# A hybrid decoder layer on one core: a first stage in program order with the statistics behind further products, and the attention heads' norm placed into the last retention projection

## The chip, the cores and the metric

The kernel runs on one core of a Trainium2 chip. The metric is the device time of one execution in microseconds (us), of which the median of several runs counts; less is better. TensorE (PE) multiplies matrices, VectorE (DVE), ScalarE (ACT) and GpSimd (POOL) work on rows of 128 partitions, and SyncE (SP) issues most of the transfers (DMA).

## The reference

All is float32: 1024 rows of 1024 columns, 16 meta rows ahead of them. Of the layer this matters here:

```python
u = rmsnorm(h, norm1_w[l])                  # over the 1024 columns
proj = u_pad @ w_in[l]                      # 1024 x 11264
rq, rk, rv, rg, dq, dk, dv, gates = jnp.split(proj, SPLIT_IDX, axis=-1)
rq = rope(rq, ...); rk = rope(rk, ...)      # 4 retention heads
ro = retention(rq, rk, rv)                  # chunks of 128, a state per head
ro = (silu(rg) * normed(ro)) @ w_ret_o[l]
dq = rope(rmsnorm(dq, q_norm_w[l]), ...)    # 8 attention heads, two halves of 64
dk = rope(rmsnorm(dk, k_norm_w[l]), ...)
do = diff_attention(dq, dk, dv, lam)
do = rmsnorm(do, diff_subln_w[l]) * (1.0 - lam_init)
do = do @ w_diff_o[l]
mix = (sigmoid(g_ret) * ro + sigmoid(g_diff) * do) @ w_out[l]
h = h + mix                                 # then a gated MLP with a convolution
```

## The kernel before, in words

Everything lies transposed, channels on the 128 partitions and up to 1040 positions along them, in groups of 346 to 348 columns (`KG`, three for 1040) or 342 (`QG`, three for 1026). Each float32 operand is split into a high and a low part of a shorter type; a product is three matmuls (high by high, high by low, low by high). A **unit** is half of a group of a projection: 12 matmuls. Weight tiles of 128 output channels come in two halves of 128x512 through a ring of three raw buffers (`raw_half`, tag `wr`); ScalarE makes the high part and GpSimd the low one (`split_half`).

*The start.* `norm_in` (L382) loads the eight input tiles `xT[k]`, multiplies each with its column of the norm's weight and splits it (`uh`, `ul`, both on VectorE), squares it on ScalarE and adds the squares up on VectorE and GpSimd. `kouter` (L198) multiplies the first two weight tiles, the keys and queries (`dk`, `dq`) of attention head 0, with input tile after input tile as they come: 8 x 18 = 144 matmuls into six accumulators. The root mean square itself is put in later: `stats` sums over partitions with TensorE, `rms` spreads the result (`rb`) and multiplies it into the rotation tables `cosr` and `sinr`, on GpSimd; the values' evacuation multiplies with `rb`. `evacuate` squares keys and queries and rotates them group by group; their own statistics go to DRAM and come back spread over the partitions. `defer(n, f)` calls `f` after n ticks, a tick being a unit or a group of `kouter`. `lam` makes a scalar from four small loads.

*The middle.* `phase1` writes the heads' steps between units of the projections (`blend`): 60 units go to each of the eight attention heads, and what is left over fills the first retention head. Head 0 begins with `prepare`, which splits keys and queries and moves halves between partitions by nine transfers that GpSimd issues. The tiles that fill are `rk`, `rq`, `rv`, `rg` and the gates, in the order of the list `fill`. `phase2` runs four retention heads, each with the output projection (`ret_out`) of the head before among its steps.

*The end of it.* The last head's `ret_out` (24 groups of 12 matmuls) runs after 2 groups and `ret_tail` (the last chunk's gate, transposes and splits). Its groups use two accumulators (`acc`), which VectorE frees by an addition (L961). `phase3` (L979) loads what the eight attention heads left in DRAM (`do`) and a row of statistics spread over the partitions, multiplies them (L990) and splits the product (ScalarE L242 and L247, the low part of odd heads on GpSimd).

The order on the engines is set by a scheduler, which takes instructions by their dependences and may move them ahead of others, except within `manual_schedule`, where they stay as written; the kernel before has no such part here.

## Time and profile before

| what | us |
|---|---|
| median of 3 runs (2581.33 to 2583.19) | 2583.08 |
| the profiled execution | 2585.65 |
| its span | 2583.9 |
| TensorE busy in the span | 2515.7 |
| VectorE, ScalarE, GpSimd busy | 1576.3, 900.5, 856.9 |
| mean granted clock of TensorE | 0.991 of full speed |

The profile follows one execution. A row of a timeline gives the start, the duration, the engine, the line of the kernel, the operation with what it writes and reads, and in brackets how long the engine had been idle and what released it. Rows of the stretches give each engine's busy time with its instructions in brackets (PE, then PEld, the loading of weights, DVE, ACT, POOL), then the mean granted clock while TensorE worked.

### The profile page before, as it was taken

The numbers are of one execution on the slowest core, as the hardware profiler recorded it, in microseconds if no ns is written. First come the engines' busy times: TensorE is split into PE (matmuls) and PEld (weight loads), VectorE is DVE, ScalarE is ACT, GpSimd is POOL, SyncE is SP. The second block draws the span as 40 slices with busy tenths as digits, with TensorE's granted clock in tenths as the row PEclk, the third lists the DMA queues.
The fourth block names the chain that finished last, engine by engine and source line by source line (L and its number), as shares of the span: only waits on it lengthen the run. The fifth ranks groups of instructions, "written<-read, shape, count | busy, mean of one in ns | idle before, by whom it ended". The sixth has DMA issues, their size and how long they took to land.

```text
span 2583.9 us, 40473 instructions
## 1 busy us (share of the span) xinstructions
PE 2515.7 (97%) x15444; PEld 2415.7 (93%) x15444; DVE 1576.3 (61%) x3239; ACT 900.5 (35%) x1881; POOL 856.9 (33%) x668
## 2 busy tenths in 40 slices
PE   7999999999999999999999998999999999999999
PEld 6888998999999999999999998999999999999998
DVE  8576766556474746453787888352466555555555
ACT  4244434354343434342556553232311111111111
POOL 4433343323232222212333432444333333332332
PEclk8999999999999999999999998999999999999999
DMA  4423141424233241424443443523111111111112
GB/s 176 104 74 98 55 130 62 127 83 115 84 89 98 68 116 55 129 78 114 116 106 89 108 104 115 175 87 115 41 50 49 42 49 50 50 41 50 50 50 86
DMA packets 171538, 224.55 MB, mean 87 GB/s; under 512 B 26712, under 2 KB 109264, under 8 KB 171344
## 3 DMA queue, kind: packets, MB, share of 16 engines
q1 hardware_dynamic: 165440, 202.70, 25.9%
q0 software_dynamic: 5760, 19.17, 3.7%
q8 instruction: 121, 1.98, 0.3%
q14 instruction: 73, 0.60, 0.1%
q10 hardware_dynamic: 144, 0.10, 0.0%
HBM read 160.20 MB, written 42.35 MB: 78 GB/s over the span
## 4 chain that ended last, share of the span: by engine, by line
PE 80%; DVE 10%; issue 4%; ACT 3%; DMA 2%; POOL 2%; SPq 0%; DVEq 0%; POOLq 0%; ACTq 0%
PE acc L175 46%; PE sc L175 26%; PE ot L175 3%; PE st L175 2%; DVE b L499 1%; PE sc L640 1%; DVE b L501 1%; ACT b L624 1%; DMA b<-d 1%; DVE b L617 1%; DVE sh L498 1%; POOL wl L230 1%; DVE b L253 1%; DVE sql L247 1%; DVE b L247 1%
## 5 line engine op out<-in xcount | busy, mean ns | idle before, releaser
L175 PE MATMUL acc<-b,wh 128*128 128x342 f32 (+3 forms) x6076 | 1481.3, 326 | 27.2 <-DVE b L961 6.8
L175 PEld LDWEIGHTS acc<-b,wh 128*128 128x128 f32 x6076 | 1055.2, 190 | 42.6 <-DVE b L961 7.4
L175 PE MATMUL acc<-b,wl 128*128 128x342 f32 (+3 forms) x3038 | 986.5, 325 | 0.3 <-POOL wl L230 0.3
L230 POOL TENSOR_TENSOR wl<-wr,wh 128x512 fp32r<-128x512 f32 x370 | 520.4, 1425 | 1044.5 <-ACT wh L227 1031.5
L175 PE MATMUL sc<-b,wh 128*128 128x342 f32 (+2 forms) x2452 | 616.7, 334 | 0.0
L175 PEld LDWEIGHTS acc<-b,wl 128*128 128x128 f32 x3038 | 576.0, 190 | 5.9 <-POOL wl L230 0.6
L175 PEld LDWEIGHTS sc<-b,wh 128*128 128x128 f32 x2452 | 433.3, 189 | 20.6 <-ACT wh L227 0.4
L227 ACT CAST wh<-wr 128x512 fp32r<-128x512 f32 x370 | 215.0, 618 | 571.9 <-issue 286.5
L175 PE MATMUL sc<-b,wl 128*128 128x342 f32 (+2 forms) x1226 | 410.3, 335 | 0.8 <-POOL wl L230 0.7
L247 POOL TENSOR_TENSOR b<-b,b 128x512 fp32r<-128x512 f32 (+2 forms) x90 | 147.5, 1639 | 320.1 <-ACT b L242 289.7
L175 PEld LDWEIGHTS sc<-b,wl 128*128 128x128 f32 x1226 | 232.1, 189 | 11.9 <-POOL wl L230 1.7
L242 ACT CAST b<-b 128x512 fp32r<-128x512 f32 (+2 forms) x135 | 100.1, 745 | 241.7 <-DVE b L1144 146.5
L534 DVE TENSOR_TENSOR ev<-acc,b 128x342 f32<-128x342 f32 (+1 forms) x144 | 74.1, 515 | 145.5 <-PE acc L175 124.9
L624 ACT ACTIVATE b<-b,sm 128x272 f32<-128x272 f32 (+7 forms) x128 | 100.9, 788 | 175.9 <-DVE sm L623 153.7
L1107 DVE SCALAR_TENSOR_TENSOR b<-b,cols,b 128x1024 f32<-128x1024 f32 x88 | 149.6, 1700 | 2.3
L617 DVE CUSTOM_DVE_ANT_0 b<-sc,consts 128x144 f32<-128x144 f32 (+6 forms) x224 | 106.6, 503 | 55.1 <-PE sc L175 54.9
L1098 DVE TENSOR_TENSOR b<-sc,b 128x342 f32<-128x342 f32 x84 | 42.5, 511 | 136.8 <-PE sc L175 136.8
L1122 DVE TENSOR_TENSOR b<-b,sc 128x512 f32<-128x512 f32 x117 | 78.6, 682 | 48.2 <-PE sc L175 48.2
L242 ACT CAST ah<-sc 128x512 fp32r<-128x512 f32 (+2 forms) x144 | 67.3, 468 | 105.2 <-PE sc L640 68.5
L247 DVE TENSOR_TENSOR al<-sc,ah 128x512 fp32r<-128x512 f32 (+2 forms) x144 | 77.3, 538 | 42.9 <-ACT ah L242 41.5
L500 POOL TENSOR_TENSOR sh<-sh,b 128x346 f32<-128x346 f32 (+1 forms) x48 | 49.9, 1040 | 152.4 <-DVE sh L498 146.2
L175 PE MATMUL sc<-b,b 128*128 128x264 f32 (+9 forms) x480 | 95.5, 317 | 4.8 <-DVE sm L617 4.7
(233 smaller groups left out, 2738.2 us busy)
## 6 DMA issues: line engine op xcount, KB each, us to landing
wr<-w_in SPq DMA_DIRECT2D x176, 256.0 KB
wr<-w_up SPq DMA_DIRECT2D x88, 256.0 KB
d<-ev SPq DMA_DIRECT2D x120, 171.0 KB
b<-b POOLq DMA_DIRECT2D x72, 260.0 KB, 4.3
b<-d SPq DMA_DIRECT2D x256, 64.0 KB
b<-d SPq DMA_DIRECT2D x24, 513.0 KB
wr<-w_down SPq DMA_DIRECT2D x44, 256.0 KB
b<-d SPq DMA_DIRECT2D x32, 260.0 KB
```

Source lines behind the costliest of these rows:

```text
L175: self.E.matmul(out, lhsT=l, rhs=r, start=start, stop=stop)
L227: self.A.copy(h, raw)
L230: self.G.tensor_sub(l, raw, h.bitcast(F32))
L242: self.A.copy(dh, src)
L247: (self.V if el == "V" else self.G).tensor_sub(dl, src, dh.bitcast(F32))
L500: G.tensor_mul(sh[:, :n], sh[:, :n], self.Sn[:, cs])
L534: V.tensor_mul(o[:, :n], ps[:, :n], self.rb[:, cs])
L617: V.tensor_tensor_reduce(out=sc_[:m, a0:a0 + sz], in0=ps[:m, :sz], in1=mk, scale=1.0, scalar=3e38, op0=ALU.add, op1=ALU.min, accum_out=sm[ ...
L624: A.activation(sc_[:m, :n], sc_[:m, :n], AF.Exp, bias=mx, scale=-1.0, accum_out=sm[:m, 10 + c:11 + c])
L1098: self.V.tensor_mul(up[:, t0:t0 + n], ps[:, :n], self.rb2[:, t0:t0 + n])
L1107: V.scalar_tensor_tensor(out=o[:, q], in0=up[:, NMETA - 2 + i:T - 2 + i], scalar=self.cw(i, fi), in1=o[:, q], op0=ALU.mult, op1=ALU.add)
L1122: self.V.tensor_add(h, h, ps)
```

## The change

`norm_in` and the first 15 units are written in the order in which they shall run. The raw weights of the first three tiles have buffers of their own; ScalarE makes the high part of seven of the inputs, VectorE the low parts of inputs and of these weights and all sums, and GpSimd has nothing to do there. `kouter` takes the first input tile's products kind by kind over its six accumulators. Keys and queries of head 0 are copied and squared on ScalarE out of the accumulators and then treated in whole rows of 1040; all statistics, rotations and `lam` are deferred behind units of the next tiles. The tiles `rv0` to `rv3` come first in the list. `prepare(0)` runs between units ahead of head 0, 5 units more follow, and a head has 58 units. The last `ret_out` has six accumulators, another order of its first six groups and `ret_tail` after four; the loads and the norm of the attention heads are written into it, and all low parts are VectorE's; `phase3` does without its loop over the heads.

```diff
+            three = lambda w: ((w[0], xh, k == 0, False), (w[0], xl, False, False), (w[1], xh, False, k == 7))
+            if k == 0:
+                order = [(three(w)[i], p, g) for i in range(3) for w, pg in zip(ws, ps) for p, g in zip(pg, groups)]
+            else:
+                order = [(t, p, g) for w, pg in zip(ws, ps) for p, g in zip(pg, groups) for t in three(w)]
+            for (w, x, b, e), p, (t0, n) in order:
+                self.mm(p[:, :n], w[:, k, :], x(k)[:, t0:t0 + n], b, e)
                 self.tick()
...
+        (self.G if el == "G" else self.V).tensor_sub(l, raw, h.bitcast(F32))
...
+        weights(0, 0, 1)
+        load(1, 2)
+        weights(4, 0, 1)
+        load(3, 4, 5, 6)
+        weights(0, 2)
+        load(7)
+        weights(4, 2)
+        self.const_loads()
+        self.C, self.Sn, self.cosr, self.sinr = (self.big() for _ in range(4))
+        for i, t in ((2, self.C), (3, self.Sn), (0, self.cosr), (1, self.sinr)):
+            S.dma_start(out=t, in_=self.a["trig"][i])
+        half = lambda b, i: self.split_half(ws[b], raws[b][:, i:i + 4, :], i, "V")
...
+        def low(k):
+            V.scalar_tensor_tensor(out=self.ul[k], in0=xs[k], scalar=self.n1[k], in1=self.uh[k].bitcast(F32),
+                                   op0=ALU.mult, op1=ALU.subtract)
+        sums = {2: [(0, 1)], 4: [(2, 3)], 5: [(0, 2)], 6: [(4, 5)], 7: [(0, 4), (0, 6)]}
...
-            self.split(uh, ul, x, eh="V", el="V", scale=self.n1[k])
...
-            A.activation(x, x, AF.Square)
-            if k == 1:
-                for w, r in zip(ws, raws[2:]):
-                    self.split_half(w, r, 4)
-            for e, i, j in {1: [(G, 0, 1)], 3: [(G, 2, 3), (G, 0, 2)], 5: [(V, 4, 5)], 6: [(V, 4, 6)],
-                            7: [(V, 4, 7), (V, 0, 4)]}.get(k, []):
-                e.tensor_add(xs[i], xs[i], xs[j])
-        self.loaded.append(self.load_w(self.stream.pop(0), [self.big(F32R)[:, :D].rearrange("p (a b) -> p a b", a=8) for _ in range(2)]))
-        self.constants()
+            if k == 0:
+                V.tensor_scalar(out=uh, in0=x, scalar1=self.n1[k], scalar2=None, op0=ALU.mult)
+                low(k)
+                half(0, 0)
+                half(1, 0)
+            else:
+                A.activation(uh, x, AF.Copy, scale=self.n1[k])
+                low(k)
+                A.activation(xs[k - 1], xs[k - 1], AF.Square)
+            if k == 2:
+                half(0, 4)
+                half(1, 4)
+            elif k == 6:
+                half(2, 0)
+            for i, j in sums.get(k, []):
+                V.tensor_add(xs[i], xs[i], xs[j])
+        A.activation(xs[7], xs[7], AF.Square)
+        half(2, 4)
+        self.const_cast()
+        V.tensor_add(xs[0], xs[0], xs[7])
...
-            x, *r = self.rstat(st, 348, 1.0 / 8, tag="x1")
+            x, *r = self.rstat(st, 348, 1.0 / 8, tag="x1", eh="V")
...
-        self.lam()
         ps = self.kouter(ws, lambda k: self.uh[k], lambda k: self.ul[k], KG)
-        self.defer(1, stats)
...
+        def trig():
             G.tensor_mul(self.cosr, self.cosr, self.rb)
             G.tensor_mul(self.sinr, self.sinr, self.rb)
...
-        self.defer(6, rms)
-        for kind, pg in zip(("dk", "dq"), ps):
-            for g in range(3):
-                self.evacuate(kind, 0, g, pg[g], KG, 4 + g//2 + 2 * (kind == "dq"))
+        kinds = ("dk", "dq")
+        raw = [self.big() for _ in kinds]
+        sq = [self.big() for _ in kinds]
+        for w, g in ((0, 0), (1, 2), (0, 1), (0, 2), (1, 0), (1, 1)):
+            t0, n = KG[g]
+            A.activation(raw[w][:, t0:t0 + n], ps[w][g][:, :n], AF.Copy, scale=self.qw if w else self.kw)
+            A.activation(sq[w][:, t0:t0 + n], ps[w][g][:, :n], AF.Square)
+        parts = [(self.big(F32R), self.big(F32R)) for _ in kinds]
+        def squares():
+            for w in range(2):
+                self.split(*parts[w], sq[w])
+        def rotate(*ws):
+            for w in ws:
+                sh = sq[w]
+                V.stream_shuffle(out=sh, in_=raw[w], mask=[(j + 8) % 16 if j < 16 else j for j in range(32)])
+                V.tensor_mul(raw[w], raw[w], self.C)
+                V.tensor_mul(sh, sh, self.Sn)
+                V.tensor_add(raw[w], raw[w], sh)
+        def stat():
+            st = self.st()
+            for w in range(2):
+                for g, (t0, n) in enumerate(KG):
+                    self.stat(st[:, :n], self.S6[2 * g + w], [t[:, t0:t0 + n] for t in parts[w]], w == 0 and g == 0, w == 1 and g == 2)
+            y = self.rstat(st, 348, eps=self.eps)
+            d = self.dram([4, T])
+            for j, (b0, m) in enumerate(KG):
+                S.dma_start(out=d[:, b0:b0 + m], in_=y[40 * j:40 * j + 40:10, :m])
+            self.ys[0] = d
+        def spread():
+            for w in range(2):
+                for r in (0, 64):
+                    S.dma_start(out=sq[w][r:r + 64, :], in_=self.ys[0][2 * w + r // 64:2 * w + r // 64 + 1, :].to_broadcast([64, T]))
+        def norm():
+            for w, kind in enumerate(kinds):
+                V.tensor_mul(raw[w], raw[w], sq[w])
+                self.raw[kind, 0] = raw[w]
+            self.normed.add(0)
+        for n, f in ((1, stats), (2, squares), (5, rms), (6, stat), (8, lambda: rotate(0)), (10, lambda: rotate(1)),
+                     (12, spread), (15, self.lam), (16, norm), (28, trig)):
+            self.defer(n, f)
...
+        fill = fill[16:20] + fill[:16] + fill[20:]
...
-        self.norm_in()
-        gen = self.projections(seq[2:])
-        units = 6 * (len(seq) - 2)
-        for _ in range(6):
+        with self.tc.manual_schedule():
+            self.norm_in()
+            gen = self.projections(seq[2:])
+            units = 6 * (len(seq) - 2)
+            for _ in range(15):
+                next(gen)
+                units -= 1
+        for _ in self.prepare(0):
             next(gen)
-        units -= 6
+            units -= 1
+        for _ in range(5):
+            next(gen)
+            units -= 1
         for h in range(DH):
-            n = 60
+            n = 58
             self.blend(self.attention(h), self.ATT_WEIGHT, gen, n)
             units -= n
...
+        last = h == RH - 1
+        order = [(m, g) for m in range(8) for g in range(3)]
+        if last:
+            order[:6] = [(0, 0), (0, 1), (1, 0), (1, 1), (0, 2), (1, 2)]
+        for m, g in order:
+            t0, n = QG[g]
+            if m % 2 == 0 and g == 0:
...
+            ps = self.acc6() if last else self.acc()
...
+        self.heads = []
+        for _ in range(4):
             next(prev)
         self.ret_tail()
-        for _ in prev:
-            pass
+        with self.tc.manual_schedule():
+            coming = [self.load_head(0)]
+            for i, _ in enumerate(prev):
+                if i % 3 == 0 and i < 20:
+                    coming.append(self.load_head(i // 3 + 1))
+                elif i % 3 == 2:
+                    self.norm_head(i // 3, *coming.pop(0))
+            while coming:
+                self.norm_head(len(self.heads), *coming.pop(0))
+    def load_head(self, h):
+        S = self.S
+        q = slice(HALO, T)
+        sp, sy = self.spill["do", h]
+        d, y = self.big(), self.big()
+        S.dma_start(out=d[:, q], in_=sp[:, q])
+        for p, n in enumerate((258, 256, 256, 256)):
+            t0 = HALO if p == 0 else NMETA + 256 * p
+            S.dma_start(out=y[:, t0:t0 + n], in_=sy[p:p + 1, :n].to_broadcast([P, n]))
+        return d, y
...
+    def norm_head(self, h, d, y):
+        q = slice(HALO, T)
+        self.V.scalar_tensor_tensor(out=d[:, q], in0=d[:, q], scalar=self.sw, in1=y[:, q], op0=ALU.mult, op1=ALU.mult)
+        a, b = self.big(F32R), self.big(F32R)
+        self.split(a[:, q], b[:, q], d[:, q])
+        self.heads.append((a, b))
...
+        dh, dl = ([t[i] for t in self.heads] for i in range(2))
+        self.heads = None
```

What stands in a row at the start of ScalarE's program, before and then after (`wh` are high parts of weights, L409 squares of inputs; in the second, L434 makes high parts of inputs, L436 squares, and `cols` are the weights of the norm):

```order
L322 DMA cols<-cols 128x195
L320 ACT_TABLE_LOAD
L320 ACTIVATE eps<-eps 128x1
L227 CAST wh_72<-wr_95 128x512
L227 CAST wh_74<-wr_97 128x512
L227 CAST wh_72<-wr_100 128x512
L227 CAST wh_74<-wr_108 128x512
L409 ACTIVATE b_76<-b_76 128x1040
```

```order
L319 ACT_TABLE_LOAD
L319 ACTIVATE eps<-eps 128x1
L321 DMA cols<-cols 128x195
L228 CAST wh_74<-b_88 128x512
L228 CAST wh_76<-b_89 128x512
L434 ACTIVATE b_141<-b_81,cols 128x1040
L436 ACTIVATE b_80<-b_80 128x1040
L434 ACTIVATE b_146<-b_82,cols 128x1040
```

The transfer of `cols` now stands behind the table load and the first activation, and high parts of inputs stand between the squares.

SyncE's transfers behind the first statistics, before and then after (`wr` are raw weights, L512 and L506 the stores of head 0's statistics, L518 and after it L512 their way back, L607 a store of the values):

```order
L430 DMA eps<-x_472 8x348
L221 DMA wr_592<-w_in 128x512
L221 DMA wr_704<-w_in 128x512
L221 DMA wr_708<-w_in 128x512
L221 DMA wr_833<-w_in 128x512
L512 DMA d_623<-ry_612 4x348
L512 DMA d_623<-ry_612 4x346 x2
L518 DMA b_654<-d_623 64x1040 x2
L518 DMA b_699<-d_623 64x1040 x2
```

```order
L462 DMA eps<-x_402 8x348
L506 DMA d_532<-ry_521 4x348
L506 DMA d_532<-ry_521 4x346 x2
L223 DMA wr_538<-w_in 128x512
L223 DMA wr_542<-w_in 128x512
L607 DMA d_571<-ev_572 128x348
L607 DMA d_571<-ev_604 128x346
L607 DMA d_571<-ev_636 128x346
L512 DMA b_354<-d_532 64x1040 x2
L512 DMA b_355<-d_532 64x1040 x2
```

The loads of raw weights stood ahead of the stores of the statistics; two of them now stand behind these stores.

VectorE's program in the last `ret_out`, before and then after (`acc` and `sc` are accumulators; L961 and after it L1043 are the additions, L913 and L990 the gate, L247 and L246 low parts, L990 and after it L1082 the product of an attention head):

```order
L961 TENSOR_TENSOR b_14508<-b_14508,acc_18118 128x342
L990 SCALAR_TENSOR_TENSOR b_18534<-b_18534,qkw,b_18535 128x1026
L961 TENSOR_TENSOR b_14508<-b_14508,acc_18132 128x342
L913 TENSOR_TENSOR vl_17882<-sc_18146,vl_17882 128x512
L247 TENSOR_TENSOR b_16868<-vl_17882,b_16864 128x128
L247 TENSOR_TENSOR b_16869<-vl_17882,b_16865 128x128
L247 TENSOR_TENSOR b_16870<-vl_17882,b_16866 128x128
L247 TENSOR_TENSOR b_16871<-vl_17882,b_16867 128x128
L961 TENSOR_TENSOR b_14508<-b_14508,acc_18160 128x342
L961 TENSOR_TENSOR b_14624<-b_14624,acc_18174 128x342
L990 SCALAR_TENSOR_TENSOR b_18546<-b_18546,qkw,b_18547 128x1026
L961 TENSOR_TENSOR b_14624<-b_14624,acc_18188 128x342
```

```order
L1043 TENSOR_TENSOR b_14580<-b_14580,sc_18116 128x342
L990 TENSOR_TENSOR vl_17838<-sc_18130,vl_17838 128x512
L246 TENSOR_TENSOR b_16824<-vl_17838,b_16820 128x128
L246 TENSOR_TENSOR b_16825<-vl_17838,b_16821 128x128
L246 TENSOR_TENSOR b_16826<-vl_17838,b_16822 128x128
L246 TENSOR_TENSOR b_16827<-vl_17838,b_16823 128x128
L1043 TENSOR_TENSOR b_14464<-b_14464,sc_18153 128x342
L1043 TENSOR_TENSOR b_14580<-b_14580,acc_18174 128x342
L1043 TENSOR_TENSOR b_14802<-b_14802,acc_18198 128x342
L1082 SCALAR_TENSOR_TENSOR b_18146<-b_18146,qkw,b_18147 128x1026
L246 TENSOR_TENSOR b_18214<-b_18146,b_18213 128x1026
L1043 TENSOR_TENSOR b_14802<-b_14802,sc_18217 128x342
```

The product of a head stood between two additions ahead of the last chunk's gate; now the gate and its four low parts come first, then three additions, then the first head's product.

## Rows read from the trace of the kernel before

**Rows 1.** The page's busy times: engine, us, share of the span, instructions.

```profile
PE 2515.7 (97%) x15444; PEld 2415.7 (93%) x15444; DVE 1576.3 (61%) x3239; ACT 900.5 (35%) x1881; POOL 856.9 (33%) x668
```

**Rows 2.** Stretches of the span: a:b, length, busy per engine, clock, DMA share, GB/s.

```profile
0.00:39.20 39.20, 29.21 (x144) 27.50 (x144) 33.56 (x27) 15.08 (x20) 19.11 (x13) 0.96 0.60 215
0.00:122.80 122.80, 100.53 (x545) 95.00 (x546) 89.31 (x116) 40.42 (x77) 59.34 (x49) 0.93 0.47 143
122.80:250.00 127.20, 117.59 (x745) 113.34 (x744) 92.48 (x233) 58.26 (x142) 47.57 (x47) 0.96 0.33 90
1572.00:1582.00 10.00, 7.21 (x24) 6.24 (x23) 7.85 (x23) 2.13 (x3) 3.70 (x3) 0.66 0.19 53
1600.00:1610.00 10.00, 7.72 (x31) 7.45 (x32) 4.30 (x8) 1.08 (x5) 2.36 (x1) 0.66 0.51 166
1602.80:1608.40 5.60, 5.55 (x19) 5.55 (x20) 1.11 (x4) 0.00 (x0) 0.00 (x0) 0.50 0.47 168
1610.00:1620.00 10.00, 10.00 (x65) 10.00 (x65) 4.65 (x7) 2.20 (x3) 2.55 (x2) 1.00 0.27 78
1620.00:1630.00 10.00, 5.98 (x28) 5.71 (x27) 2.13 (x3) 1.05 (x1) 2.38 (x1) 0.79 0.39 134
```

**Rows 3.** TensorE's waits, 0 to 123 us: waited for, total us, times, longest.

```profile
PE acc L175 <- DVE b L252: 6.4, 1, 6.4
...
PE acc L175 <- ACT x L471: 4.4, 1, 4.4
...
PE ot L175 <- DVE ryl L253: 1.4, 1, 1.4
```

**Rows 4.** The same view of 123 to 250 us.

```profile
PE sc L640 <- DVE b L631: 4.4, 2, 3.8
PE sc L676 <- DVE sm L617: 2.8, 1, 2.8
```

**Rows 5.** VectorE's timeline, 1565 to 1645: start, us, instruction, idle before it.

```profile
1569.97 4.17 DVE L247 TENSOR_TENSOR b<-x,b 128x128 fp32r<-128x128 f32 x4
...
1600.51 2.88 DVE L247 TENSOR_TENSOR b<-vl,b 128x128 fp32r<-128x128 f32 x4 [0.36 <-ACT b L242]
...
1624.67 1.29 DVE L990 SCALAR_TENSOR_TENSOR b<-b,qkw,b 128x1026 f32<-128x1026 f32 x1 [5.48 <-DMA b<-d]
```

**Rows 6.** SyncE's own timeline, 1570 to 1665.

```profile
1619.83 3.42 SPq L989 DMA_DIRECT2D b<-d  x4
```

**Rows 7.** ScalarE's timeline, 0 to 9 us (ACTq: a transfer that it issues).

```profile
0.74 0.41 ACTq L322 DMA_DIRECT2D cols<-cols  x1
1.18 1.28 ACT L320 ACT_TABLE_LOAD   x1 [1.18 <-PEq L1201]
```

**Rows 8.** VectorE's timeline, 0 to 104 us.

```profile
5.16 0.17 DVE L364 TENSOR_SCALAR qkw<-cols 128x3 f32<-128x3 f32 x1 [3.19 <-DMA cols<-cols]
...
13.33 2.21 DVE L253 SCALAR_TENSOR_TENSOR b<-b,cols,b 128x1040 fp32r<-128x1040 f32 x1
...
18.45 1.30 DVE L253 SCALAR_TENSOR_TENSOR b<-b,cols,b 128x1040 fp32r<-128x1040 f32 x1
...
68.24 2.63 DVE L282 SCALAR_TENSOR_TENSOR sq<-sq 128x348 f32<-128x348 f32 x1
...
74.69 0.52 DVE L283 SCALAR_TENSOR_TENSOR ry<-sq,ry 128x348 f32<-128x348 f32 x1
```

**Rows 9.** ScalarE by line and shape, 0 to 123: total us, mean ns.

```profile
L409 ACT ACTIVATE b<-b 128x1040 f32<-128x1040 f32 x8 | 8.5, 1070 | 15.1 <-DVE b L253 15.1
```

**Rows 10.** SyncE's timeline, 60 to 110 us.

```profile
75.24 1.87 SPq L512 DMA_DIRECT2D d<-ry  x3
```

**Rows 11.** GpSimd's timeline, 0 to 104 us.

```profile
67.88 2.62 POOL L444 TENSOR_TENSOR b<-b,b 128x1040 f32<-128x1040 f32 x1 [2.64 <-ACT b L457]
...
89.63 0.70 POOL L571 DMA_DIRECT2D b<-b  x1
```

**Rows 12.** TensorE's waits, 1560 to 1660 us.

```profile
PE acc L175 <- DVE b L961: 6.8, 2, 4.0
```

More of the change, by code (lines that the diff above doesn't have):

```diff
@@ L362, in lam @@
         a, cp, S, V, A, pc = self.a, self.cp, self.S, self.V, self.A, self.pc
-        qkw = cp.tile([P, 3], F32, name="qkw")
-        V.tensor_scalar(out=qkw, in0=pc[:, 16:19], scalar1=1 / RS, scalar2=None, op0=ALU.mult)
-        self.qw, self.kw, self.sw = (qkw[:, i:i + 1] for i in range(3))
-        V.tensor_scalar(out=self.qw, in0=self.qw, scalar1=-0.125, scalar2=None, op0=ALU.mult)
-        V.tensor_scalar(out=self.sw, in0=self.sw, scalar1=0.8, scalar2=None, op0=ALU.mult)
         lm = self.big()[:, :256].rearrange("p (a b) -> p a b", a=4)
@@ L385, in norm_in @@
         self.uh, self.ul = [], []
[L386 to L387 removed]
+        blks = [self.stream.pop(0) for _ in range(3)]
+        ws = [self.tile_w() for _ in range(2)]
+        ws.append([self.big(F32R)[:, :D].rearrange("p (a b) -> p a b", a=8) for _ in range(2)])
         xs = [self.big() for _ in range(8)]
+        raws = [self.big()[:, :D].rearrange("p (a b) -> p a b", a=8) for _ in blks]
         def load(*ks):
@@ L392, in load, with weights @@
                 S.dma_start(out=xs[k], in_=self.a["xT"][k])
+        def weights(i, *bs):
+            for b in bs:
+                S.dma_start(out=raws[b][:, i:i + 4, :], in_=blks[b][:, i:i + 4, :])
         self.setup()
         load(0)
-        raws = [self.raw_half(b, 0) for b in blks]
-        load(1)
-        raws.append(self.raw_half(blks[0], 4))
-        load(2, 3)
-        for w, r in zip(ws, raws):
-            self.split_half(w, r, 0)
-        raws.append(self.raw_half(blks[1], 4))
@@ L981, in phase3 @@
         q = slice(HALO, T)
-        dh, dl = [], []
-        for h in range(DH):
-            sp, sy = self.spill["do", h]
-            d, y = self.big(), self.big()
-            S.dma_start(out=d[:, q], in_=sp[:, q])
-            for p, n in enumerate((258, 256, 256, 256)):
-                t0 = HALO if p == 0 else NMETA + 256 * p
-                S.dma_start(out=y[:, t0:t0 + n], in_=sy[p:p + 1, :n].to_broadcast([P, n]))
-            V.scalar_tensor_tensor(out=d[:, q], in0=d[:, q], scalar=self.sw, in1=y[:, q], op0=ALU.mult, op1=ALU.mult)
-            a, b = self.big(F32R), self.big(F32R)
-            self.split(a[:, q], b[:, q], d[:, q], el="G" if h % 2 else "V")
-            dh.append(a)
-            dl.append(b)
+        dh, dl = ([t[i] for t in self.heads] for i in range(2))
+        self.heads = None
         gates = {}
```

84 lines of the change are left out of this document (36 added, 48 removed).

## The prediction

> **What bounds the kernel now.** I read the busy shares first: TensorE is busy for 2515.7 of 2583.9 us [rows 1], so the time is its work plus what it loses. The change leaves TensorE's program as long as it was (15,066 rows, before and after), so nothing can come but from lost time. The stretches of the span came next. An undisturbed stretch of the last retention projection holds 65 matmuls in 10.00 us, 0.154 us each for 342 columns [rows 2]; 348 columns then take 0.157. The first 545 matmuls would need 545 x 0.157 = 85.6 us and end at 122.8 [rows 2]: 37.2 us are lost there. 22.3 of them are idle time (122.8 - 100.5 busy), the rest is slow running: at a granted clock of 0.50 (1.2 of 2.4 GHz), 19 matmuls took 5.6 us [rows 2], 0.292 each, and such a spell follows every longer idle time. From 122.8 to 250 the engine idles 127.2 - 117.6 = 9.6 us. At the last retention head's end three slices of 10 us hold 24, 31 and 28 matmuls [rows 2], so they lose 6.3 + 5.2 + 5.7 = 17.2 us.
>
> The waits say for whom. At the start: 6.4 us for the first normalised input, 4.4 for a copy on ScalarE, 1.4 for a split's low part [rows 3]. In the first attention head: 4.4 and 2.8 us for statistics of the scores [rows 4]; that head has few projections left to fill it, because preparing it has used them up. At the end: VectorE waits 5.48 us for a transfer ahead of additions that free the two accumulators [rows 5], and the transfers' issues stand on SyncE [rows 6].
>
> **The change part by part.** A, the start, by walking through the new order.
>
> First matmul. Before, the transfer of the columns is issued at 0.74, ahead of the table load (1.28 us from 1.18) [rows 7], and lands at 5.16 [rows 8]. Now it stands behind the table load and the activation, so it is issued 1.9 later and lands near 7: the first matmul moves from 6.4 to about 8.2. Bounds +1 and +2.5; I take +1.8.
>
> The 144 matmuls of the first two weight tiles. They ended at 39.2 [rows 2], 33 us for 22.6 us of work, because VectorE made both parts of each input and GpSimd ran beside it: the low part took 2.21 us beside GpSimd and 1.30 without [rows 8]. Now ScalarE makes seven high parts, eight squares and six weight halves (0.5 of a 1040-wide step each): 18 x 1.07 = 19 us [rows 9]. VectorE makes one high part, eight low parts, six weight halves at half a step, seven sums and a split of two, all near 1.30 with GpSimd silent: 1.3 x (1 + 8 + 3 + 7 + 2) = 27 us from 7.2, so done at 34.5. Both stay ahead of TensorE, by little at the very end, where the statistics' operand is wanted at 35. So TensorE sets the pace: 8.2 + 144 x 0.157 = 30.8, and 19 matmuls at 0.292 rather than 0.157 add 2.6: the stage ends at **33.4**, not 39.2.
>
> The 401 matmuls after it, 63.0 us of work. The statistics now run behind products of the next tile, so the waits of [rows 3] go. What is late next: the broadcast through one bank with two ScalarE copies between (the nearest row is the 1.4 us wait; I take 1.9, bounds 0 and 4.4, the row of the ScalarE wait); the values' weights, whose two SyncE issues now stand behind three stores that wait for the attention statistics (such stores were issued at 75.2 for 1.87 us [rows 10]; SyncE holds up nothing else that is due) and the evacuations, which stand on VectorE between the eight rotation steps of 1.3 (one group's evacuation behind four of them is 5.2 us, about three groups' PE time of 3 x 24 x 0.157 is 11, so two accumulators cover most): 1.6 at the first of these tiles, 1.8 in it, 0.7 at the next. Together 6.0. The 545th matmul then ends at 33.4 + 63.0 + 6.0 = 102.4, a gain of **20.4** (bounds 12, if three of the stalls also bring a slow spell of 2.6, and 26, if no stall is left). The multiplications of the tables on GpSimd, which took 2.62 us and stretched a VectorE step beside them from 0.52 to 2.63 [rows 8, 11], are put behind the 28th unit, where only a retention tile's evacuation asks for them; if that cover were gone, two such steps would cost 4.2.
>
> B, the first attention head. Its preparation now runs between projections before the head's steps, and the head keeps its full filler. Of 9.6 us idle I take **5** as gained; bounds 0 (the waits are on VectorE's statistics, not on filler) and 10.
>
> C, the other heads. 58 units rather than 60 and other tiles in them: the same work in another place, **0**, bounds -5 and +5 (one wait of 4.4, as in [rows 4], more or less). D, the first retention head has 21 rather than 30 units left to fill it: **-1**, bounds -4 and 0, from the same row.
>
> E, the end. Six accumulators instead of two mean that an addition which comes late by 5.48 us [rows 5] stops nothing: 12 matmuls are 1.9 us, and the four further groups give 7.5. The first head's normalisation no longer stands among the last chunk's splits, nor does GpSimd run its halves: the four splits of 128 columns that took 4.17 and 2.88 us [rows 5] go back to a few tenths each (128 of 1040 columns, and a 1040-wide step takes 1.3). VectorE then has, per three groups (5.7 us of TensorE), three additions of about 0.5 (the 0.52 of a step as wide [rows 8]), the product of 1.29 [rows 5] and a low part that can't be dearer: 4.1, which fits; the odd heads' low parts are four of these. Left over: about 1.2 us behind the last chunk's transposes, a slow spell of 2.6, and 1 for the last head, whose loads stand behind weight loads that wait for GpSimd, together 4.8. So 17.2 - 4.8 = **12.4**, bounds 8 and 17.
>
> The sum: 20.4 + 5 + 0 - 1 + 12.4 = 36.8, about 37. The profiled execution took 2585.65 us with a span of 2583.9, and lies 2.6 over the median of 2583.08; I take the gain off the median: 2583.08 - 37 = **2546**. With the terms' bounds taken as independent, it is 24 to 50 less: 2533 to 2559.
>
> **The rivals.** *The start gives half of it back.* VectorE is the fullest engine there (89.3 of 122.8 us busy [rows 2]) and now has the rotations in 1040-wide steps in front of evacuations. If each of the four stalls is followed by a slow spell, 4 x 2.6 = 10.4 go, and if the values' weights land one issue later, a few us more: 2556 to 2566. Against it: two accumulators and TensorE's 3.8 us per group.
>
> *The queue of GpSimd's transfers.* Preparing the first head issues nine transfers on GpSimd, now beside rotations and evacuations. Before, one took 0.70 us with VectorE busy beside it [rows 11]. If they were held as a VectorE step was beside GpSimd (2.63 - 0.52 = 2.1 [rows 8]), the chain would be 9 x 2.1 = 19 us longer, nearly all before the first scores: some 17 us, so 2563. The row of 0.70 speaks against it. The Trainium skill, page "SBUF — State Buffer", section "A bandwidth-pool intuition that's wrong (but worth ruling out)", says that a GpSimd-issued transfer of about 620 ns takes about 3100 ns beside a VectorE copy, since its descriptors wait for a shared port; by that figure the estimate would be 9 x 2.5 = 22 us. The 0.70 us of this trace doesn't bear that out so far.
>
> *The end keeps its waits.* SyncE issues the heads' transfers between weight loads; four of them took 3.42 us there from 1619.83 [rows 6], and the product that needed them began at 1624.67 [rows 5]. If two heads are late as one was at 1624.7, 2 x (4.0 [rows 12] + 2.6) = 13 are lost again: 2559.
>
> *Slower: thinner filler.* Every head has 58 units for steps paced for 60, and the weights in them have moved. If a head's statistics stop TensorE as in the first head (one wait of 3.8 [rows 4] and a slow spell of 2.6), it costs 6.4 a head, 51 for eight: 2597. It decides from 37/8 = 4.6 us a head. Against it: two units are 7.5 us in a head of 110, and the first head, with far less filler, lost 9.6.
>
> *It doesn't do what it says.* The scheduler may still place other instructions (a multiplication of the later normalisation) into the hand-made order, and the first matmul's cause, a transfer, remains: near 2583.
>
> **How the numbers follow.** The forecast, a gain of 21 to 50, has 0.74; the start giving half back 0.07; the queue 0.03; the end 0.05; better than 50, 0.02; no effect 0.04; slower 0.05. About 5 us, 0.2%, is what a measurement can tell from no change. Faster: 0.74 + 0.07 + 0.03 + 0.05 + 0.02 = 0.91; same 0.04; slower 0.05. The range takes the forecast's own bounds from 2533 and reaches up to the first three rivals, 2564.
>
> **What would show it.** Right: the first matmul near 8.2, the 144th ended near 33.4, the 545th near 102; no wait over 2 us in the statistics; 62 to 65 matmuls in nearly every slice of 10 us of the last projection; no GpSimd work before 30 us. Wrong: low parts still above 2 us at the start; first scores later than 110; a wait for the statistics of scores in every head; a wait for the additions or the last heads' split at the end.

## The result and the profile after

The changed kernel takes 2567.26 us (median of 4 runs, 2566.07 to 2568.86) against 2583.14 for the one before: a ratio of 0.994, with an interval of 0.9926 to 0.9955, or **15.9 us** less. Forecast were 37, with a range of 19 to 50; the direction was right and the size was not. The profiled execution took 2568.86 us, its span 2567.1.

The busy shares of the changed kernel, where [rows 1] stood before:

```profile
PE 2509.6 (98%) x15444; PEld 2416.9 (94%) x15444; DVE 1550.9 (60%) x3228; ACT 904.0 (35%) x1881; POOL 816.8 (32%) x649
```

The stretches of its span (length, busy time and instructions of PE, PEld, DVE, ACT, POOL, clock, DMA share, GB/s), as in [rows 2]:

```profile
0.00:34.80 34.80, 25.56 (x145) 25.59 (x146) 25.73 (x31) 22.31 (x27) 0.20 (x4) 1.00 0.74 280
0.00:108.80 108.80, 94.13 (x546) 92.03 (x547) 72.12 (x101) 43.74 (x73) 27.52 (x29) 0.97 0.54 166
1580.00:1590.00 10.00, 8.89 (x57) 8.50 (x57) 4.06 (x11) 2.43 (x7) 2.54 (x2) 1.00 0.55 181
1590.00:1600.00 10.00, 10.00 (x65) 10.00 (x65) 4.86 (x6) 2.19 (x3) 2.54 (x2) 1.00 0.55 177
1600.00:1610.00 10.00, 10.00 (x66) 10.00 (x65) 6.86 (x10) 3.25 (x4) 2.53 (x2) 1.00 0.64 219
1610.00:1620.00 10.00, 10.00 (x65) 10.00 (x64) 7.96 (x10) 2.19 (x3) 2.53 (x2) 1.00 0.10 29
1620.00:1630.00 10.00, 10.00 (x66) 10.00 (x65) 4.65 (x7) 3.14 (x4) 2.29 (x2) 1.00 0.43 132
1630.00:1640.00 10.00, 9.54 (x61) 9.26 (x59) 4.62 (x5) 1.05 (x1) 0.26 (x1) 1.00 0.75 257
```

The 144th matmul has ended by 34.8 us rather than 39.2, and the 545th starts at 108.8 rather than 122.8; the five slices of the last retention projection, 1580 to 1630, hold 57, 65, 66, 65 and 66 matmuls (61 in the next, behind its last addition), where three slices held 24, 31 and 28. So both ends of the change did what they were meant to do. To see what became of the rest, I took the distance between the starts of neighbouring matmuls, less the median distance of the same shape in the trace of before, and added it up by the number of the matmul. This is time lost, whatever the engine waits for, and it can be compared where the order of the matmuls has changed. For the kernel before and the changed one there are two profiled executions each (the second ones are experiments, below):

| stretch, by matmul | before | again | after | again | gain forecast | gain, first profiles |
|---|---|---|---|---|---|---|
| up to the first | 6.4 | 6.5 | 9.2 | 9.4 | | |
| 1 to 144 | 11.7 | 11.7 | 2.6 | 2.3 | | |
| 145 to 545 | 18.4 | 18.8 | 10.4 | 10.8 | A: 20.4 | 14.3 |
| to 1450, first head | 18.2 | 17.3 | 13.3 | 14.9 | B: 5 | 4.9 |
| to 7600, other heads | 25.1 | 25.2 | 33.8 | 28.5 | C: 0 | -8.7 |
| to 9400, retention | 7.0 | 7.2 | 8.7 | 8.9 | D: -1 | -1.7 |
| to 10400, its end | 20.4 | 13.8 | 6.6 | 6.6 | E: 12.4 | 13.8 |
| to 15443, later stages | 1.6 | 1.7 | 7.3 | 7.3 | 0 | -5.7 |

(A is the sum of the first three rows.) The gains add up to 16.9, the difference of the spans (16.8) but for rounding. 37 was missed in three places: the start, the heads behind the first, and the later stages, which the change doesn't touch.

### The profile page after: what moved, and what is told of

Its sections match the earlier page's. It is cut to its first block, busy times and chain, and to the rows that moved or that the text cites. A ratio compares the mean times of both kernels' runs of the same rounds, so it can differ in the third digit from the quotient of the medians.

```text
span 2567.1 us, 40420 instructions
## 1 busy us (share of the span) xinstructions
PE 2509.6 (98%) x15444; PEld 2416.9 (94%) x15444; DVE 1550.9 (60%) x3228; ACT 904.0 (35%) x1881; POOL 816.8 (32%) x649
## 5 line engine op out<-in xcount | busy, mean ns | idle before, releaser
L175 PE MATMUL acc<-b,wh 128*128 128x342 f32 (+3 forms) x5948 | 1451.0, 326 | 15.7 <-DVE b L429 9.2
L175 PEld LDWEIGHTS acc<-b,wh 128*128 128x128 f32 x5948 | 1033.7, 190 | 28.4 <-issue 9.2
L175 PE MATMUL acc<-b,wl 128*128 128x342 f32 (+3 forms) x2974 | 966.9, 325 | 1.5 <-POOL wl L229 1.5
L229 POOL TENSOR_TENSOR wl<-wr,wh 128x512 fp32r<-128x512 f32 x366 | 507.6, 1404 | 1148.8 <-ACT wh L228 1136.5
L175 PE MATMUL sc<-b,wh 128*128 128x342 f32 (+2 forms) x2580 | 648.6, 334 | 1.1 <-ACT b L241 1.1
L175 PEld LDWEIGHTS sc<-b,wh 128*128 128x128 f32 x2580 | 455.2, 189 | 22.5 <-ACT b L241 1.3
L175 PE MATMUL sc<-b,wl 128*128 128x342 f32 (+2 forms) x1290 | 429.3, 334 | 0.0
L246 POOL TENSOR_TENSOR b<-b,b 128x512 fp32r<-128x512 f32 (+1 forms) x86 | 138.3, 1608 | 304.9 <-ACT b L241 262.7
L241 ACT CAST b<-b 128x512 fp32r<-128x512 f32 (+3 forms) x137 | 102.1, 750 | 214.0 <-DVE b L1242 145.6
L246 DVE TENSOR_TENSOR al<-sc,ah 128x512 fp32r<-128x512 f32 (+2 forms) x144 | 77.6, 539 | 68.3 <-ACT ah L241 68.0
L241 ACT CAST ah<-sc 128x512 fp32r<-128x512 f32 (+2 forms) x144 | 67.3, 467 | 121.8 <-PE sc L709 84.0
L1203 DVE TENSOR_SCALAR b<-b,cols 128x1024 f32<-128x1024 f32 x44 | 81.5, 1853 | 1.6
```

Of the source, the lines that this page charges most:

```text
L175: self.E.matmul(out, lhsT=l, rhs=r, start=start, stop=stop)
L229: (self.G if el == "G" else self.V).tensor_sub(l, raw, h.bitcast(F32))
L241: self.A.copy(dh, src)
L246: (self.V if el == "V" else self.G).tensor_sub(dl, src, dh.bitcast(F32))
L1203: V.tensor_scalar(out=o[:, q], in0=up[:, q], scalar1=self.cw(2, fi), scalar2=self.cb(fi), op0=ALU.mult, op1=ALU.add)
```

## The experiments

Each time is compared with runs of the kernel before on the same chip; "lost" is by the table above.

**Each kernel once more.** No edit; one profile each.

> The kernel before, unchanged, profiled once more. In the changed kernel's trace the matmuls of 342 columns after the last retention projection, a stretch that the change does not touch, are 157.8 ns apart in the mean, against 156.8 in the trace of before, which over the last 940 us makes some 7 us. Theory 'the execution': this is how one profiled execution (or one chip) differs from another, and the new trace of the same kernel shows a value between 156.8 and 157.8, and a span that moves with it by some us. Theory 'the layout': buffers lie elsewhere in the changed kernel and its matmuls are slower for it; then this trace shows 156.8 again.

> The changed kernel, unchanged, profiled once more. The second profile of the kernel before repeated 156.8 ns for 342 columns in the last stages to the tenth. Theory 'the layout' (a property of the program): 157.8 ns again here. Theory 'the execution': another value, such as the 157.0 and 157.2 of the two halves of the change. The heads' loss after the first head, about 10 us against before, should repeat at the same rows if it comes from the order.

The spans were 2577.4 and 2563.9. From matmul 10400 to the last, before took 871.47 and 871.52 us, the changed kernel 877.14 and 877.10, and the undisturbed matmuls of 342 columns from the 11400th on were 156.76, 156.76, 157.81 and 157.81 ns apart. So the rate is a property of the program and repeats. It isn't the whole of the 5.6 us between them: distances over 40 ns longer than the median add up to 3.9 and 3.8 us in the changed kernel's two executions and to 2.3 in both of before, so 1.6 us are stops, and some 4 are the rate. TensorE's longest wait in the changed kernel's 1660 to 2600 us, which before doesn't have:

```profile
PE st L175 <- ACT b L241: 1.7, 1, 1.7
```

This stop, too, stands in both executions, and in the run of the start alone; the run of the end alone doesn't have it. That "the layout" sets the rate wasn't shown: no buffer was moved by itself. The second thing: in the end of the retention, the same kernel lost 20.4 us in one execution and 13.8 in the other. TensorE's waits there, 1560 to 1710 us, first in the execution of [rows 12], then in the other:

```profile
PE acc L175 <- DVE b L961: 6.8, 2, 4.0
...
PE sc L911 <- ACT on L797: 0.6, 1, 0.6
```

```profile
PE acc L175 <- DVE b L961: 5.3, 2, 2.8
PE sc L911 <- ACT on L797: 2.3, 1, 2.3
```

The stops for the additions were shorter, another was longer, and the slow spells, which I had put into the sum as part of the price, were mostly missing: between 1570 and 1633 us the granted clock was 0.50 for 20.5 us in the first execution and for 3.4 in the other.

**The start alone and the end alone.** The changed kernel with `ret_out`, `phase2` and `phase3` of before; and the kernel before with those three of the change.

> The changed start, the new order of the tiles, the preparation between units and 58 units a head; the last retention projection and the norm of the attention heads as before. The changed trace was 13.9 us ahead at the 545th matmul, 18.5 after the first head, and 8.7 at the end of the other heads. Theory 'the heads give it back': 8 to 9 us less than before. Theory 'the loss in the heads is one execution's accident': 16 to 19 less.

> The kernel before with the changed end alone: six accumulators, the order of the first six groups, the gate after four units, the loads and the norm of the attention heads within the last retention projection. By my sum 12.4 us less than before; by the changed trace, 15 less at the end of the projection. Theory 'the layout slows the last stages', if it comes with the end: 15 less at the projection's end, 8 at the program's end. Theory 'the execution': 13 to 15 less.

The start alone takes 2574.18 against 2582.71 (0.9967, 0.9955 to 0.998), 8.5 us less; the end alone 2572.01, 10.7 less (0.9955, 0.9942 to 0.9969), between its two forecasts. The start alone loses 34.0 in heads 1 to 7, as the changed kernel does, so the heads do give it back, and the end has no part in that. The end alone loses 5.5 where before lost 20.4 or 13.8. In the later stages they lose 4.1 and 3.7, both together 7.3.

**60 units a head.**

```diff
-            n = 58
+            n = 60
```

> The changed kernel with 60 units a head rather than 58, so that the first retention head has 5 units left rather than 21. Theory 'thinner filler' (my rival for the slower side): the heads lose 9 us less, and the first retention head a few more, so 5 to 9 us less than the changed kernel. Theory 'the order of the tiles': the stops stand where the retention's key and query tiles fall, whatever the number of units: within 3 us of the changed kernel.

2579.66 us against 2582.71 (0.9986, 0.9977 to 0.9994): 3.1 less, where the changed kernel has 15.9: slower by some 13 us, which neither theory had. The heads lose 33.5, as with 58. What it costs is the retention behind them: 29.0 lost instead of 8.7, as the first retention head has 5 units left. So my rival "thinner filler" falls for the attention heads, and stands for the retention head: 16 units fewer cost 20 us there. TensorE's waits in that stretch, 1180 to 1370 us of this kernel:

```profile
PE sc L988 <- ACT on L874: 8.3, 6, 2.4
```

**The retention's keys and queries first again.**

```diff
-        for n, f in ((1, stats), (2, squares), (5, rms), (6, stat), (8, lambda: rotate(0)), (10, lambda: rotate(1)),
-                     (12, spread), (15, self.lam), (16, norm), (28, trig)):
+        for n, f in ((1, stats), (2, squares), (5, rms), (6, stat), (7, trig), (8, lambda: rotate(0)), (10, lambda: rotate(1)),
+                     (12, spread), (15, self.lam), (16, norm), ):
...
-        fill = fill[16:20] + fill[:16] + fill[20:]
```

> The changed kernel with the retention's key and query tiles first again, as before, and the multiplication of the rotation tables at the 7th tick rather than the 28th, since these tiles need it. Theory 'the order of the tiles costs the heads 10 us': heads 1 to 7 lose no more than before, 8 to 10 us come back there; at the start GpSimd's two multiplications and the rotations' evacuations cost VectorE 4 to 8. In sum 0 to 6 us less than the changed kernel. Theory '58 units cost the heads 10 us': the heads lose as in the changed kernel, and the sum is 4 to 8 us more than the changed kernel.

2564.51 against 2582.47 (0.9931, 0.9919 to 0.9944): 18.0 less than before, which is not clear of the changed kernel's 15.9. The heads behind the first lose 25.2, as much in sum as before, with 58 units a head. So **the order of the tiles costs the heads 3 to 9 us** (28.5 and 33.8 in the two executions; in every trace with the new order 28.5 to 34.6, in every one with the old 25.1 to 25.2). The start pays for it: 24.9 lost up to the 545th rather than 22.2, and the first head loses 3 more. At the start GpSimd now multiplies the tables beside the rotations; on VectorE, 60 to 74 us of this kernel's timeline, steps of 1.24 took up to 3.48, the first rows below; the last row is GpSimd's first multiplication:

```profile
60.69 1.24 DVE L496 TENSOR_TENSOR b<-b,b 128x1040 f32<-128x1040 f32 x1
...
64.81 2.31 DVE L495 TENSOR_TENSOR b<-b,b 128x1040 f32<-128x1040 f32 x1
67.16 3.33 DVE L496 TENSOR_TENSOR b<-b,b 128x1040 f32<-128x1040 f32 x1
70.41 3.48 DVE L516 TENSOR_TENSOR b<-b,b 128x1040 f32<-128x1040 f32 x1
```

```profile
65.99 3.40 POOL L473 TENSOR_TENSOR b<-b,b 128x1040 f32<-128x1040 f32 x1
```

**Every tile five units later.** The loop of five units behind `prepare(0)` is left out.

> The changed kernel without the five units between the preparation and the first head, so that every tile falls five units later on the heads' steps, at the same 58 units a head and the same order of tiles; the first retention head has 26 units left. Theory 'too few units in a head': the heads lose what they lose in the changed kernel, some 7 to 11 us behind the first. Theory 'where the evacuations fall on the steps': the stops move to other places and their sum changes by more than 3 us, up or down; the stop of 8.5 us at the third head's begin, between the matmuls 2400 and 2900, goes or halves.

2559.32 against 2581.17 (0.9913, 0.9899 to 0.9926), 21.9 less. The sum of heads 1 to 7 hardly moved (32.8), and the matmuls 2400 to 2900 lost 10.5, against 12.5 and 10.2 in the changed kernel's two traces: there my theory of where evacuations fall on steps, in its form of a mere shift, got no support. The gain lies in the first head, which lost 4.6 rather than 13.3: its waits of 123 to 250 us had been, in the changed kernel and then here:

```profile
PE ot L175 <- DVE al L246: 3.5, 2, 1.8
PE sc L709 <- DVE b L700: 3.2, 1, 3.2
```

```profile
PE sc L709 <- DVE b L700: 1.2, 1, 1.2
PE st L175 <- ACT sqh L241: 1.1, 1, 1.1
```

**The columns first.** The transfer of `cols` is put ahead of the activation in `setup`.

> The changed kernel with the transfer of the norm's columns issued ahead of the table load and the first activation on ScalarE, as before. It landed at 8.0 where it is issued at 2.0, and at 5.2 where it was issued at 0.74. Theory 'the first matmul waits for it alone': the first matmul at 6.4 instead of 9.2, and 2 to 3 us less than the changed kernel. Rival 'inputs come at their own rate': the second input lands at 8.4 whatever the columns do, so that TensorE stops after the first 18 matmuls, and 0 to 1 us are won.

2565.55 against 2582.47 (0.9928, 0.9914 to 0.9941), 16.9 less, no measurable difference from the changed kernel. The first matmul started at 6.8 and the 545th 2.5 us earlier, but the first head then lost 15.3 rather than 13.3: most of it had been given back by the 900th matmul. Here the gain at the start didn't outlast the first head; why, no run shows.

**Two tiles' stores on ScalarE.**

```diff
-            S.dma_start(out=self.spill[kind, i][:, cs], in_=o[:, :n])
+            (A if kind == "rv" and i < 2 else S).dma_start(out=self.spill[kind, i][:, cs], in_=o[:, :n])
```

> The changed kernel with the stores of the first two value tiles issued by ScalarE instead of SyncE. In the changed trace three of these stores hold SyncE for 9.6 us from 61.6, since they wait for evacuations behind the rotations; the spread of the statistics and the weights of the third value tile stand behind them, and TensorE waits 2.1 us for these weights at 78.5 and runs slowly after it. Theory 'SyncE's queue is that stop': no wait for weights at 78.5, the 386th matmul at 77 to 79 instead of 81.4, and 3 to 6 us less. Rival 'VectorE sets it': the evacuations themselves come late, the stop at 63 stays and the one at 78 turns into a wait for them: within 2 us.

2563.93 against 2582.47 (0.993, 0.9918 to 0.9943), 18.5 less; by this alone it can't be told from the changed kernel's 15.9; the trace shows more. The matmul that the forecast means (the 387th) starts at 78.5 instead of 81.4, and the stretch to the 545th loses 6.8 instead of 10.4. SyncE's timeline of the changed kernel, and ScalarE's cast that waits for the weights:

```profile
58.74 1.82 SPq L506 DMA_DIRECT2D d<-ry  x3
60.60 0.91 SPq L223 DMA_DIRECT2D wr<-w_in  x2
61.61 9.62 SPq L607 DMA_DIRECT2D d<-ev  x3
71.33 2.96 SPq L512 DMA_DIRECT2D b<-d  x4
74.38 1.00 SPq L223 DMA_DIRECT2D wr<-w_in  x2
```

```profile
80.31 1.20 ACT L228 CAST wh<-wr 128x512 fp32r<-128x512 f32 x2 [15.27 <-DMA wr<-w_in]
```

The first two loads behind the stores of the statistics are what my sum had in it (1.6 us). What it had missed are the rows behind them in the same piece of the order: three stores of the values (L607) hold SyncE for 9.62 us, until the evacuations behind the rotations are done, and the spread (L512) and the **next** tile's weights stand behind these. TensorE's wait at the changed kernel's 81 us, and with the stores on ScalarE all its waits from 55 to 110:

```profile
80.98 0.90 PE L175 MATMUL acc<-b,wh 128*128 128x348 f32 x4 [2.15 <-ACT wh L228]
```

```profile
PE acc L175 <- DVE ev L606: 2.6, 2, 1.4
PE acc L175 <- POOL wl L229: 1.1, 2, 0.7
```

The wait for the cast is gone, the evacuations' one has grown by 1.4. In the changed kernel a slow spell stands behind that wait, at a granted clock of 0.51:

```profile
83.30:86.70 3.40, 3.40 (x14) 3.40 (x13) 2.67 (x8) 1.74 (x5) 2.21 (x4) 0.51 0.84 237
```

From the 384th matmul on, the stop and its spell cost 4.7 us in the changed kernel (3.1 and 1.5) and 1.2 with the stores on ScalarE. These 3.5 us stay through the heads.

**Two accumulators at the end.**

```diff
-            ps = self.acc6() if last else self.acc()
+            ps = self.acc()
```

> The changed kernel with two accumulators instead of six in the last retention projection, the order of its work otherwise as changed. My sum laid the end's 12 us on the accumulators, on the gate behind four groups, and on the heads' norm in its place. Theory 'the accumulators carry it': stops of 2 to 4 us for the additions come back, and 5 to 10 us more than the changed kernel. Theory 'the place of the norm carries it': VectorE is never late by more than a group of 1.9 us, and it is within 2 us of the changed kernel. Besides, the spacing of the matmuls of 342 columns in the last stages (157.8 ns in the changed kernel) shows whether the choice of accumulators sets it.

2568.09 against 2581.17 (0.9945, 0.9933 to 0.9958), 13.1 less than before, where the changed kernel was 15.9 less: 2.8 us, between the two forecasts, with intervals that overlap. In the trace the end loses 7.7 rather than 6.6. TensorE's waits there, 1540 to 1660 us, of the changed kernel and of this one:

```profile
PE acc L175 <- ACT b L241: 2.9, 1, 2.9
```

```profile
PE acc L175 <- DVE b L1043: 4.1, 4, 1.4
PE acc L175 <- ACT b L241: 1.1, 1, 1.1
```

With two accumulators it stops four times for an addition, by 1.4 at most, where before had two stops, by up to 4.0 [rows 12]. So most of the end's gain doesn't come from the accumulators. What carries it, the place of the norm, the gate behind four groups or the low parts on VectorE, no run takes apart. The rate in the later stages stayed slow (158.0 ns), so the accumulators don't set it.

**What the runs point to.** The columns first, the stores on ScalarE, and the loads of the last four heads one to four groups earlier:

```diff
-                if i % 3 == 0 and i < 20:
-                    coming.append(self.load_head(i // 3 + 1))
-                elif i % 3 == 2:
+                if i in (0, 3, 6, 8, 10, 12, 14):
+                    coming.append(self.load_head(1 + (0, 3, 6, 8, 10, 12, 14).index(i)))
+                if i % 3 == 2:
```

> The changed kernel with three edits: the columns' transfer first on ScalarE, the stores of the first two value tiles issued by ScalarE, and the loads of the last four attention heads issued one to four groups earlier. The first two won 0.6 and 6.2 us of the span alone; the last head's product waits 4.28 us for its transfer and TensorE 2.9 for its high part at 1639. If the three add up: 2567 less 3 to 4 for the stores, 0 to 2 for the columns, 3 for the loads, 2558 to 2561. If SyncE only moves the wait to the weights of the next stage: 2562 to 2565.

> The three edits together, and the five units between the preparation and the first head left out as well. The three gave 26.4 us against before, leaving out the five units 21.9, and the changed kernel 15.9. Theory 'the stops in the heads are set by where the tiles fall, whatever the start does': the two add up, 10.5 + 6.0 beyond the changed kernel, 2549 to 2553. Theory 'both win the same wait of the first head': 2554 to 2558.

2554.78 against 2581.17 (0.9894, 0.9879 to 0.9909): 26.4 less, 3 us more than the better forecast. (That forecast gave the columns 0.6 us of the span and the stores 6.2; the spans are 2567.6 and 2561.4 against 2567.1, so the columns alone had won nothing and the stores 5.7.) The earlier loads took the last wait of the end away: VectorE's product of the last head in the changed kernel, and then here:

```profile
1640.01 1.29 DVE L1082 SCALAR_TENSOR_TENSOR b<-b,qkw,b 128x1026 f32<-128x1026 f32 x1 [4.28 <-DMA b<-d]
```

```profile
1625.85 1.28 DVE L1082 SCALAR_TENSOR_TENSOR b<-b,qkw,b 128x1026 f32<-128x1026 f32 x1
```

Without the five units as well it takes **2549.58** against 2581.14 (0.9873, 0.9856 to 0.9889): 31.6 less. By the medians the two add up (10.5 + 6.0 beyond the changed kernel, and 15.7 measured). Where the gain lies isn't shown: the profiled execution, 2553.82, is the slowest of its four and no shorter than that of the three edits (2553.15). In it the first head loses 4.9 rather than 13.2, but the stretch ahead of it 12.3 rather than 7.0, as TensorE now waits 3.0 us for one of the preparation's transfers, and the other heads 34.6 rather than 30.4.

## Why the prediction was wrong, and where it was right

**A, the start: 14.3 instead of 20.4.** The first matmul started at 9.24 instead of 8.2: I moved the transfer's issue and kept its duration, 4.4 us, but issued at 2.00, behind three of SyncE's loads, it took 6.0 (in the run with the columns first, issued at 0.73, 4.9). ScalarE's and VectorE's timelines of the changed kernel:

```profile
2.00 0.41 ACTq L321 DMA_DIRECT2D cols<-cols  x1
```

```profile
8.01 0.17 DVE L328 TENSOR_SCALAR qkw<-cols 128x3 f32<-128x3 f32 x1 [6.05 <-DMA cols<-cols]
...
11.55 2.51 DVE L420 SCALAR_TENSOR_TENSOR b<-b,cols,b 128x1040 fp32r<-128x1040 f32 x2
```

The 144 matmuls went as forecast: ended at 34.8 for 33.4, of which 1.0 is the late first one; the low parts take 1.25 each without GpSimd, and no stop is left. The stops behind it cost 10.4 us instead of 6.0. By their places: 1.8 for the statistics (forecast 1.9), 3.9 at and in the second value tile (1.6 + 1.8), and 4.7 at the third, with its slow spell, instead of 0.7. That one waits for its weights behind the values' stores. The step that failed is "SyncE holds up nothing else that is due": the stores held SyncE for 9.62 us, and the row of the order that says so stands ahead of the prediction. I followed the queue to the first load that stands behind the wait, and not to the next.

**B, the first head: 4.9 for 5.** Right in size by the first profiles; with the second ones it is 2.4 to 4.9, so the match is partly luck. That the filler is the cause is not shown: leaving out five units gave 8.7 more there.

**C, the other heads: -8.7 (-3.4 in the second execution) instead of 0.** "The same work in another place, 0" was the step that failed. It isn't the number of units, as the run with 60 shows, but the order of the tiles. In the changed kernel the retention's keys and queries come four tiles later in the list, and more of them meet the third head. TensorE's waits of 250 to 1020 us, before and after:

```profile
PE sc L640 <- DVE b L631: 7.7, 6, 2.7
PE sc L175 <- DVE sm L617: 4.7, 5, 0.9
PE ot L175 <- DVE al L247: 3.0, 5, 0.8
```

```profile
PE sc L709 <- DVE b L700: 14.2, 11, 3.1
PE st L175 <- DVE sql L246: 2.7, 2, 2.5
PE sc L175 <- DVE sm L686: 1.9, 2, 1.3
PE st L175 <- ACT sqh L241: 1.4, 1, 1.4
```

In sum they are 15.4 us before and 20.2 after. Head by head, the third one (taken as the matmuls 2330 to 3207) loses 4.1 and 4.2 us in the two traces of before and 3.1 with the old order, where none of these tiles is evacuated in it; in the two of the changed kernel it loses 12.7 and 10.4, where six groups of them are.

VectorE and GpSimd at the longest stop, 440.6 to 444.0 us, where TensorE waits for L700:

```profile
439.79 1.44 DVE L246 TENSOR_TENSOR sql<-sq,sqh 128x258 fp32r<-128x258 f32 x1
441.15 0.75 DVE L698 TENSOR_TENSOR sm<-sm,nl 128x1 f32<-128x1 f32 x1
441.82 0.50 DVE L550 TENSOR_TENSOR sh<-acc,b 128x346 f32<-128x346 f32 x1
442.25 0.50 DVE L551 TENSOR_TENSOR ev<-acc,b 128x346 f32<-128x346 f32 x1
442.70 1.25 DVE L700 SCALAR_TENSOR_TENSOR b<-b,sm,b 128x528 f32<-128x528 f32 x1
```

```profile
439.39 1.55 POOL L229 TENSOR_TENSOR wl<-wr,wh 128x512 fp32r<-128x512 f32 x1 [1.27 <-ACT wh L228]
440.90 0.98 POOL L552 TENSOR_TENSOR ev<-x,b 128x346 f32<-128x346 f32 x1
```

L550 to L555 are the evacuation of one of these tiles. Beside GpSimd's weight half and its share of the evacuation, a low part of 258 columns takes 1.44 us, a scalar column 0.75 and the product that TensorE waits for 1.25; the medians of the same steps in this trace are 0.42, 0.16 and 0.77. These 2.1 us and the two evacuation steps of 0.50 between them add up to the stop of 3.1. That such meetings are the whole cost of the heads was only read; that the order brings the cost is shown by the run with the old order, 25.2, though there the heads have their losses in other places than before and only the sum is the same.

**D: -1.7 for -1**, within its bounds. **E, the end: 13.8 for 12.4** by the first profiles, 7.2 by the second of before; the run of the end alone gave 10.7. The size holds, the reason only half: six accumulators are worth about 1 us in the trace, and which of the gate's place, the norm's place and VectorE's low parts brought the rest is open. The wait for the last head's loads came where the prediction had it (2.9 us for 1 and a slow spell).

**The later stages: -5.7**, of which no step spoke. They hold the same work, and I took it that the same work takes the same time. Some 4 us are the spacing of the matmuls, whose cause is open, and 1.6 a stop for a high part (L241), which comes with the changed start.

**Of the rivals**, the start giving half of it back came true in part, 6.1 of 20.4 us, of which 4.0 are the late weights of a value tile with a slow spell behind them; at the end one wait of 2.9 returned instead of two heads' waits; thinner filler is refuted for the heads. The queue of GpSimd's transfers stayed short: two of the nine, in the changed kernel beside VectorE's splits,

```profile
83.47 0.70 POOL L643 DMA_DIRECT2D b<-b  x1
85.22 0.52 POOL L644 DMA_DIRECT2D b<-b  x1 [1.05 <-DVE l L379]
```

are as short as in [rows 11]. The rule of the Trainium skill, page "SBUF — State Buffer", section "A bandwidth-pool intuition that's wrong (but worth ruling out)", by which a transfer that GpSimd issues takes about 3100 ns beside a VectorE copy, is neither borne out nor refuted by these rows, nor by that of [rows 11]: what VectorE did beside them were subtractions of two operands (the low parts), not copies.

**Readings that were off.** The spacing of 0.154 us for 342 columns was a count of a slice; the starts are 0.157 apart, and 0.159 for 348, which adds 1 us to the work of 545 matmuls. The slow spell doesn't follow every longer stop: in the trace of before itself none stands behind a stop of 2.85 us at 409 us. The gate moved behind two further groups (3.8 us), not four. Two units are 24 matmuls, 3.8 us and not 7.5, in heads that take 134 to 140 us behind the first, not 110. The terms' bounds, taken as independent, give 25 to 47 us less, not 24 to 50.

**The sum was too sure of one execution.** I subtracted what one profile lost, 2.6 us above the median, from the median; a second profile of the same kernel shows 6.6 us less lost in one of the three stretches on which the sum rests.

## What to carry to other kernels

When a step is moved on a queue, follow everything behind it until the first instruction that doesn't mind, the second tile's loads too; and when work is handed from one stage to another, "the same work elsewhere" is an estimate with a sign, to be priced in the stage that takes it. A transfer's duration belongs to its place among other transfers, and a stop's price, with the slow spell behind it, should come from two executions. Where the time is nearly all TensorE's, keep some range for the stages that the change doesn't touch.

## What the runs showed of the hardware that I had not expected

The spacing of the same matmuls of 342 columns in untouched stages (from the 11400th on) went from 156.8 to 158.0 ns over the programs of this case, and the two programs that were profiled twice kept theirs (157.81 to 157.83 in the changed kernel, its repetition, with the columns first and with the stores on ScalarE; 157.0 and 157.2 in its two halves, 156.9 with 60 units, 157.1 with the old order). Over these stages it's up to 5 us, and what sets it stays open.

Whether a slow spell follows a stop is a matter of the execution. In the end of the retention the same kernel had stops of 1.6 to 4.2 us in one and of 1.6 to 2.9 in the other, and 20.5 and 3.4 us at a granted clock of 0.50.

The first matmuls of the changed kernel ran slowly too, from 9.24 to 14.58, 18 of them 0.297 us apart, as in the slow spell of [rows 2]. No row shows the granted clock there: in this execution its records begin at 14.97 us, where the slow spacing has ended.
